# A decoder layer on one core: six gate loads, the operands around the FFN, and the last rows' statistics put elsewhere

## The chip, the core and the metric

The kernel runs on one core of a Trainium2 chip. The core has five engines that work from queues of their own: TensorE (PE, matmuls, into banks of PSUM), VectorE (DVE), ScalarE (ACT), GpSimd (POOL) and SyncE (SP), which only starts transfers; POOL starts transfers too. An instruction waits in its queue until its operands and its buffers are free, and what stands behind it on that engine waits with it. The metric is device time of the whole program in microseconds.

## What is computed

One decoder layer on x of 2048 rows by 1024 columns, float32:

```python
proj = x @ w_in                       # 4872 columns, split among the heads and gates
y_a = sliding_window_attention_with_sinks(aq, ak, av, sinks) @ w_attn_out
o = gated_delta_rule_chunked(dq, dk_, dv_, g, beta)      # behind a conv and SiLU
y_b = (rms_norm(o) * dn_norm_w * silu(dz)) @ w_dn_out
mix = (sigmoid(g_a) * y_a + sigmoid(g_b) * y_b) @ w_out
x = layer_norm(alpha * x + mix)                          # ln1
h = square(relu(x @ w_up)) @ w_down                      # 4096 hidden columns
x = layer_norm(alpha * x + h)                            # ln2
```

## The kernel before

Every matmul operand is split into a high and a low part: ScalarE copies the raw tile to the rounded type (hi), VectorE subtracts that from the raw tile (lo, called a remainder here). A product is then three matmuls per block, hi by hi, hi by lo, lo by hi.

Tokens go through in four quarters of 512. **Stage A** makes the projections, attention and the delta rule of all quarters, and stores y inputs (ya, yb) and gates (tg) to DRAM. The **y stage** takes a quarter at a time in eight blocks m of 128 columns; each has two products of 12 matmuls (L147). `prepare` loads ya and yb (L982), `load_y` a block's weights w (L1044, L1045), both on SP's queue for the first quarter; the two gates of a block come by POOL (L1021). VectorE multiplies by the gates, and L1100 is the product with w_out. `turn_rows` and `norm_steps` make ln1 and its transpose.

The **FFN's first half** is a loop over two token halves s and 16 pairs p of 128-column blocks. A pair is one level of a Strassen-like scheme: seven products n = 0 to 6 of 12 matmuls each (L1392) into the banks X, Z, X, Y, X, Z, X, on the sums T1 to T4 and blocks B11 to B22 of the tokens and sums S1 to S4 and blocks of the weights. n = 0, 1, 3 begin a bank anew, the others add on it. After n = 0, 1, 2 `keep` (L1348) copies the bank to SBUF, and the next product on the bank can't start before that copy is done. After n = 3 to 6 `out_block` (L1355 to L1357) adds, applies relu and squares. `h_sums` (L1368 to L1377) makes four sums S1 to S4 of a pair's blocks, and `store` (L1361) writes blocks and sums to DRAM (h). `x_operand` loads, copies and splits a token operand (L945, L950, L953); `up_weights` does that for weights and their sums (L1124 to L1157).

The **down stage** has groups g of hidden columns and, inside, four token quarters tq, again with seven products (L1518); each is added to the rows in SBUF by `add` (L1465), and the bank it reads is free after that. `hidden` loads what the first half stored (L1215), copies (L1222) and splits (L1226); `down_operand` does so for w_down (L1266 or L1268, L1271, L1273) through raw buffers lng, lnb and dr. In the last group `norm_out` (L1471 to L1487) makes ln2 of the rows of a quarter with ScalarE's accumulations and POOL's power and add; the last two rows of the last quarter go through `norm_steps` (L872 to L884) instead.

From the FFN on, the order on every engine is the order of the code. Helpers are generators: `go_on` advances each one in the list `ahead` by a step after every product, so the place where a helper enters `ahead` decides which instructions stand before and behind its own. In the stages before, PE's order is by code, and that of the others by priorities.

## Time and profile before

| what | us |
|---|---|
| median of three runs (2818.43 to 2823.88) | 2819.61 |
| profiled execution | 2823.9 |
| its span | 2822.2 |
| PE busy in it | 2744.7 |
| VectorE busy | 1916.0 |
| ScalarE busy | 1202.7 |
| POOL busy | 688.0 |

The profiled execution is the slowest of the three. PE is busy almost throughout, so the places to read are those where it stands, what releases it there, and the clock it is granted afterwards. Between stages the engines hand over to each other, and a share over the whole span doesn't show that; the timeline around a place does.

### The profile page before, as it was taken

How to read it: one execution, taken by the hardware profiler on the slowest of the kernel's cores; microseconds unless marked ns; L12 is line 12 of the kernel's file. 1: busy time of each engine (PE TensorE's matmuls, PEld its weight loads, DVE VectorE, ACT ScalarE, POOL GpSimd, SP SyncE). 2: the span in 40 equal slices, each digit the busy share in tenths (PEclk: the TensorE clock that was granted, in tenths of full speed). 3: DMA queues.
4: the chain of work that ended last, by engine and by line, in shares of the span. 5: the costliest groups of instructions: out<-in, count | busy, mean ns of one | idle time of the engine just before them, and what ended most of it. 6: DMA issues, size and time to landing. Idle time of an engine off the chain costs nothing. (4 is left out here: it accounts for less than half of the span.)

```text
span 2822.2 us, 37859 instructions
## 1 busy us (share of the span) xinstructions
PE 2744.7 (97%) x13509; PEld 2263.3 (80%) x13509; DVE 1916.0 (68%) x3032; ACT 1202.7 (43%) x2406; POOL 688.0 (24%) x913
## 2 busy tenths in 40 slices
PE   8999999999999999999999999999999999999996
PEld 6878888888888888788878788878887888888874
DVE  6875666466645674566766866698865777777787
ACT  4545443444344434323323555565555322223345
POOL 1022202230223032213462124448730000000015
PEclk9999999999999999999999999999999999999998
DMA  6785556354634464857787567789975644444443
GB/s 211 235 278 188 213 172 209 130 188 168 211 135 178 169 205 136 242 193 261 255 274 246 175 215 236 247 284 301 302 242 185 248 152 153 129 134 152 146 143 137
DMA packets 355083, 569.91 MB, mean 202 GB/s; under 512 B 42208, under 2 KB 236880, under 8 KB 354896
## 3 DMA queue, kind: packets, MB, share of 16 engines
q1 hardware_dynamic: 313616, 426.97, 46.5%
q0 software_dynamic: 41280, 140.54, 14.0%
q8 instruction: 106, 1.74, 0.2%
q14 instruction: 81, 0.66, 0.1%
HBM read 391.22 MB, written 176.19 MB: 201 GB/s over the span
## 5 line engine op out<-in xcount | busy, mean ns | idle before, releaser
L329 PE MATMUL pj<-x,w 128*128 128x512 f32 x3648 | 930.4, 399 | 4.6 <-DVE qs L723 2.5
L329 PEld LDWEIGHTS pj<-x,w 128*128 128x128 f32 x3648 | 662.3, 189 | 128.9 <-issue 2.9
L1518 PE MATMUL X<-x,w 128*128 128x512 f32 x1536 | 369.5, 393 | 13.7 <-DVE st L1477 7.0
L1392 PE MATMUL X<-x,w 128*128 128x512 f32 x1536 | 368.4, 392 | 12.1 <-ACT c L1348 11.7
L1518 PEld LDWEIGHTS X<-x,w 128*128 128x128 f32 x1536 | 290.0, 190 | 78.4 <-issue 14.5
L1392 PEld LDWEIGHTS X<-x,w 128*128 128x128 f32 x1536 | 289.7, 189 | 74.5 <-ACT c L1348 13.3
L1222 ACT ACTIVATE w<-w 128x1024 fp32r<-128x1024 f32 x96 | 101.5, 1058 | 251.8 <-DMA w<-h 251.8
L1136 DVE TENSOR_TENSOR w<-w,w 128x512 fp32r<-128x512 f32 x224 | 174.3, 789 | 16.2 <-ACT w L1132 15.9
L1392 PE MATMUL Z<-x,w 128*128 128x512 f32 x768 | 185.2, 390 | 0.0
L147 PE MATMUL b<-x,w 128*128 128x512 f32 x768 | 181.4, 396 | 3.2 <-ACT w L110 2.6
L1518 PE MATMUL Z<-x,w 128*128 128x512 f32 x768 | 184.4, 389 | 0.0
L111 DVE TENSOR_TENSOR w<-w,w 128x1024 fp32r<-128x1024 f32 x102 | 127.9, 1254 | 82.1 <-PE b L1100 44.0
L110 ACT ACTIVATE w<-w 128x1024 fp32r<-128x1024 f32 x102 | 107.8, 1057 | 171.1 <-DMA w<-in_w_dn_out_dram 84.7
L1478 POOL TENSOR_TENSOR st<-st,mh 128x1 f32<-128x1 f32 x14 | 7.6, 556 | 683.1 <-DVE st L1477 683.1
L147 PEld LDWEIGHTS b<-x,w 128*128 128x128 f32 x768 | 145.3, 191 | 33.8 <-ACT w L110 2.9
L1392 PEld LDWEIGHTS Z<-x,w 128*128 128x128 f32 x768 | 144.3, 188 | 30.0
L1518 PEld LDWEIGHTS Z<-x,w 128*128 128x128 f32 x768 | 144.2, 188 | 29.9
L1132 ACT ACTIVATE w<-w 128x512 fp32r<-128x512 f32 x224 | 135.9, 621 | 62.4 <-DVE w L1142 33.6
L1465 DVE SCALAR_TENSOR_TENSOR x<-x,X 128x1024 f32<-128x1024 f32 x96 | 117.0, 1219 | 66.1 <-PE X L1518 66.1
L1100 PE MATMUL b<-w,x 128*128 128x512 f32 x512 | 159.4, 392 | 0.0
L1226 DVE TENSOR_TENSOR w<-w,w 128x1024 fp32r<-128x1024 f32 x96 | 122.4, 1275 | 12.3 <-ACT w L1222 12.3
L414 DVE SCALAR_TENSOR_TENSOR acc<-cin,cw,acc 128x512 f32<-128x512 f32 x144 | 114.3, 794 | 15.9 <-ACT acc L412 13.5
(326 smaller groups left out, 4361.9 us busy)
## 6 DMA issues: line engine op xcount, KB each, us to landing
w<-whd SPq DMA_DIRECT2D x114, 512.0 KB, 3.3
w<-wld SPq DMA_DIRECT2D x114, 512.0 KB, 4.6
h<-c SPq DMA_DIRECT2D x224, 256.0 KB, 4.4
w<-h SPq DMA_DIRECT2D x96, 512.0 KB, 3.5
w<-in_w_up_dram SPq DMA_DIRECT2D x64, 512.0 KB, 5.5
w<-in_w_in_dram SPq DMA_DIRECT2D x38, 512.0 KB, 4.4
whd<-w SPq DMA_DIRECT2D x38, 512.0 KB, 3.1
wld<-w SPq DMA_DIRECT2D x38, 512.0 KB, 5.1
```

Source lines behind the costliest of these rows:

```text
L110: A.activation(hi, raw, AF.Copy)
L111: V.tensor_tensor(lo, raw, hi, ALU.subtract)
L147: PE.matmul(pp, lhsT=a[:, k0 + k, :], rhs=b[k // 4][:, k % 4, :], start=n == 0, stop=n == 3 * nk - 1)
L329: PE.matmul(pp, lhsT=a[:, k, :], rhs=b[k // 4][:, k % 4, :], start=n == 0, stop=n == 23)
L414: V.scalar_tensor_tensor(acc, cin[:, j:j + TQ], cw[:, 12 * j + gi:12 * j + gi + 1], acc, ALU.mult, ALU.add)
L1100: PE.matmul(accs[tb], lhsT=a[:, kg, ts_], rhs=b[:, k, :], start=kg == 0 and n == 0, stop=kg == 7 and n == 2)
L1132: A.activation(t[:, 0, :], src, AF.Copy)
L1136: V.tensor_tensor(l, raw[name], h, ALU.subtract)
L1226: V.tensor_tensor(parts[1], raw_, parts[0], ALU.subtract)
L1392: PE.matmul(dst, lhsT=l[:, ks], rhs=r[:, xs], start=first and k == 0 and m == 0, stop=k == 3 and m == 2, skip_group_check=not first)
L1465: V.scalar_tensor_tensor(dst, dst, 1.0 if (tq, half, ch) in touched else ALPHA, bank, ALU.mult, ALU.add)
L1518: PE.matmul(dst[:, j], lhsT=l[:, ks], rhs=r[:, k], start=first and k == 0 and m == 0, stop=k == 1 and m == 2, skip_group_check=not first)
```

## The change

Six places change. In the y stage of the first quarter, the gates of blocks 0 to 2 are loaded by SP, behind the weights of their block, instead of by POOL. In the FFN's first pair, operand B22 is loaded into four 128x512 tiles of the tag "c" in place of two 128x1024 slots of the weights, and T4 is copied a step later. The four sums of the pairs (0, 14) and (1, 15) are made by POOL, as those of (0, 15) were already. The first `hidden` of the down stage and its operands 0 to 5 enter `ahead` one product earlier. In the last quarter, all four row tiles take their statistics with bn_stats and go through `norm_steps`, and each is stored in two halves; `norm_out` loses its case for the end.

```diff
--- before.py
+++ after.py
@@ -940,7 +940,8 @@
         src = x_source(s, name)
         hi, lo = (t[:, i].rearrange("p k t -> p (k t)") for i in range(2))
         dst[name] = (hi, lo)
-        parts = [(raw, slice(i * D, i * D + D)) for i, raw in enumerate(raws)]
+        w = raws[0].shape[-1]
+        parts = [(raw, slice(i * w, i * w + w)) for i, raw in enumerate(raws)]
         for raw, cs in parts:
             q.dma_start(raw, src[:, cs])
         yield
@@ -1005,6 +1006,18 @@
                 A.activation(xt, ps_, AF.Copy)
                 G.dma_start(x1t_d[s][:, kh, th, :, tb * P:tb * P + P], xt)
 
+        def y_weights(m):
+            ms = slice(m * P, (m + 1) * P)
+
+            def load_y(raw):
+                wa = w_attn.rearrange("(j t d) c -> j d t c", j=2, t=4)
+                for j in range(2):
+                    nc.sync.dma_start(raw[64 * j:64 * j + 64, 0:4, :], wa[j][:, :, ms])
+                loads.append(nc.sync.dma_start(raw[:, 4:8, :], w_dn[:, ms].rearrange("(k p) c -> p k c", p=P)))
+
+            with (tc.issue_after(loads[-1].ins) if len(loads) < 20 else nullcontext()):
+                return weights(None, [NK, P], load=load_y)
+
         for q in range(NQ):
             t0 = q * TQ
             ys = ready
@@ -1018,8 +1031,14 @@
                 for i in range(2):
                     th = tgs[:, tgn % 6, :]
                     tgn += 1
-                    lastg = G.dma_start(th, tg_d[q][:, i * NK + m, :])
+                    if q > 0 or m > 2:
+                        lastg = G.dma_start(th, tg_d[q][:, i * NK + m, :])
                     gates.append(th)
+                wy = y_weights(m) if q == 0 else None
+                if q == 0 and m < 3:
+                    with tc.issue_after(loads[-1].ins):
+                        for i, th in enumerate(gates):
+                            loads.append(nc.sync.dma_start(th, tg_d[q][:, i * NK + m, :]))
                 if q == 0 and m == 6:
                     with tc.issue_after(lastg.ins):
                         G.dma_start(gt, ln1_g[0].partition_broadcast(P))
@@ -1036,16 +1055,7 @@
                 if lastq:
                     next(sums, None)
                     next(sums, None)
-                ms = slice(m * P, (m + 1) * P)
...
-                with (tc.issue_after(loads[-1].ins) if q == 0 and m >= 2 else nullcontext()):
-                    wh, wl = weights(None, [NK, P], load=load_y)
+                wh, wl = wy or y_weights(m)
                 for i in range(2):
                     yh, yl = ys[i]
                     pp = new(ps, [P, TQ], "b", 6)
@@ -1258,16 +1268,16 @@
         name = RIGHT[i]
         o = dn[0] % 8
         dn[0] += 1
-        while len(dx) <= o // 2:
-            dx.append(xslot(len(dx), (2, 2, 2, TQ)))
-        t = dx[o // 2][:, o % 2]
-        dst[name] = (t[:, 0], t[:, 1])
         if name in SUMS:
             nc.sync.dma_start(raw, wsum_d[g][:, SUMS[name]])
         else:
             nc.sync.dma_start(raw, wd[g][int(name[1]) - 1][int(name[2]) - 1])
         yield
         yield
+        if len(dx) <= o // 2:
+            dx.append(xslot(len(dx), (2, 2, 2, TQ)))
+        t = dx[o // 2][:, o % 2]
+        dst[name] = (t[:, 0], t[:, 1])
         A.activation(t[:, 0], raw, AF.Copy)
         yield
         V.tensor_tensor(t[:, 1], raw, t[:, 0], ALU.subtract)
@@ -1312,11 +1322,12 @@
 
         run(up_weights(0, all_wops[0]))
         load_up(1)
-        for name in ("B22", "T4"):
-            ahead.append(x_operand(0, name, xops[0], [flat(slot(F32)) for _ in range(2)], nc.sync, 2))
+        ahead.append(x_operand(0, "B22", xops[0], [new(sb, [P, TQ], "c", 11) for _ in range(4)], nc.sync, 2))
+        ahead.append(x_operand(0, "T4", xops[0], [flat(slot(F32)) for _ in range(2)], nc.sync, 3))
         go_on()
         side = side_work()
         part = None
+        GP = {(0, NP - 2), (0, NP - 1), (1, NP - 1)}
 
         halves, places = [], []
         BEGIN = [1, 2, 2, 3, 3, 4, 5, 5, 6, 7, 8, 9, 10, 11]
@@ -1363,7 +1374,7 @@
 
                 store = storing()
 
-                def h_sums(h=h, store=store, eng=G if turn_over else V):
+                def h_sums(h=h, store=store, eng=G if (s, p) in GP else V):
                     s1 = tile_c()
                     eng.tensor_tensor(s1, h["A21"], h["A22"], ALU.add)
                     store("S1", s1)
@@ -1397,10 +1408,8 @@
                     for _ in range(BEGIN.count(at)):
                         ahead.append(halves.pop(0))
                     go_on()
-                    if n == 0:
-                        ahead.append(hidden(0, 0, hops) if final else loaded.pop(0))
-                        if final:
-                            next(ahead[-1])
+                    if n == 0 and not final:
+                        ahead.append(loaded.pop(0))
                     if n == 6 and s * NP + p + 2 < 2 * NP:
                         load_up(s * NP + p + 2)
 
@@ -1429,12 +1438,13 @@
                         next(side, None)
                     elif part != "turn" and n < 6:
                         part = next(side)
-                    if final:
-                        if n == 0:
-                            lnc = [new(lnpool, [P, D], "lng", 1), new(lnpool, [P, D], "lnb", 1)]
-                        for i in {0: (0, 1), 3: (2, 3), 6: (4, 5)}.get(n, ()):
-                            ahead.append(down_operand(0, i, bops, lnc[i % 2].rearrange("p (k c) -> p k c", k=2)))
-                            next(ahead[-1])
+                    if at == 7 * NP - 1:
+                        ahead.append(hidden(0, 0, hops))
+                        next(ahead[-1])
+                        lnc = [new(lnpool, [P, D], "lng", 1), new(lnpool, [P, D], "lnb", 1)]
+                    for i in {-1: (0, 1), 2: (2, 3), 5: (4, 5)}.get(at - 7 * NP, ()):
+                        ahead.append(down_operand(0, i, bops, lnc[i % 2].rearrange("p (k c) -> p k c", k=2)))
+                        next(ahead[-1])
                 if final:
                     for steps in after:
                         run(steps)
@@ -1465,7 +1475,7 @@
             V.scalar_tensor_tensor(dst, dst, 1.0 if (tq, half, ch) in touched else ALPHA, bank, ALU.mult, ALU.add)
             touched.add((tq, half, ch))
 
-        def norm_out(r, t, end):
+        def norm_out(r, t):
             junk = new(sb, [P, D], "dr", 5)
             st_ = new(lnt, [P, 4], "st", 4)
             A.activation(junk, r, AF.Copy, accum_out=st_[:, 0:1])
@@ -1477,16 +1487,13 @@
             V.tensor_scalar(st_[:, 3:4], st_[:, 2:3], 1.0 / D, LN_EPS, ALU.mult, ALU.add)
             G.tensor_tensor(st_[:, 3:4], st_[:, 3:4], mh, ALU.pow)
             yield
-            if end:
-                V.scalar_tensor_tensor(r, junk, st_[:, 3:4], bt_, ALU.mult, ALU.add)
-                nc.sync.dma_start(out[t * P:t * P + P, :], r)
-                return
             A.activation(junk, junk, AF.Copy, scale=st_[:, 3:4])
             yield
             G.tensor_tensor(r, junk, bt_, ALU.add)
             ST.dma_start(out[t * P:t * P + P, :], r)
             yield
 
+        norms_ = []
         load_acc(0)
         for g in range(NG):
             bo = bops
@@ -1503,7 +1510,7 @@
                 end = last and tq == 3
                 tl = tiles_of(tq)
                 banks = {"X": new(ps, [P, 2, TQ], "X", 2), "Y": new(ps, [P, 2, TQ], "Y", 1), "Z": new(ps, [P, 2, TQ], "Z", 1)}
-                stats = [new(lnt, [P, 2, 6], f"bl{j}", 1) for j in range(2)] if end else None
+                stats = [new(lnt, [P, 2, 6], f"bl{j}", 1) for j in range(4)] if end else None
                 for n, (a, b, bank) in enumerate(SEVEN):
                     if a not in ho or b not in bo:
                         go_on()
@@ -1524,19 +1531,20 @@
                     add(tq, *((0, 0), (1, 1), (0, 1), (0, 0), (1, 1), (0, 1), (1, 0))[n], dst)
                     if g == 0 and tq < 3 and n == 1:
                         load_acc(tq + 1)
-                    if last and n == 5:
-                        ahead += [norm_out(acc[tq][:, j, :], tl[j], end) for j in range(2)]
-                    if end and n == 4:
+                    rows_ = [acc[tq][:, j, :] for j in range(4)]
+                    if last and not end and n >= 5:
+                        ahead += [norm_out(rows_[2 * (n - 5) + j], tl[2 * (n - 5) + j]) for j in range(2)]
+                    if end and n >= 3:
                         for j in range(2):
-                            V.bn_stats(stats[j][:, 1, :], acc[tq][:, 2 + j, TQ:])
-                    if last and n == 6:
-                        for j in range(2):
-                            r, t = acc[tq][:, 2 + j, :], tl[2 + j]
-                            if end:
-                                V.bn_stats(stats[j][:, 0, :], r[:, 0:TQ])
-                                ahead.append(norm_steps(r, gt, bt_, mh, out[t * P:t * P + P, :], stats[j], True))
-                            else:
-                                ahead.append(norm_out(r, t, end))
+                            half, ch = ((0, 0), (1, 1), (0, 1), (1, 0))[n - 3]
+                            V.bn_stats(stats[2 * half + j][:, ch, :], rows_[2 * half + j][:, ch * TQ:ch * TQ + TQ])
+                    if end and n >= 5:
+                        for j in range(2 * (n - 5), 2 * (n - 5) + 2):
+                            t = tl[j]
+                            if n == 6:
+                                run(norms_.pop(0))
+                            norms_.append(norm_steps(rows_[j], gt, bt_, mh, out[t * P:t * P + P, :], stats[j], True))
+                            next(norms_[-1])
                     if g == 0 and tq == 0 and n == 0:
                         ahead.append(down_operand(0, 6, bo, new(sb, [P, 2, TQ], "dr", 5)))
                         next(ahead[-1])
@@ -1545,8 +1553,9 @@
                         if i is not None:
                             ahead.append(down_operand(g + 1, i, bops, new(sb, [P, 2, TQ], "dr", 5)))
                             next(ahead[-1])
-        while ahead:
-            go_on()
+        assert not ahead
+        for steps in norms_:
+            run(steps)
 
 
 _INS = ["x", "w_in", "conv_w", "attn_sinks", "dn_a_log", "dn_dt_bias", "dn_norm_w", "w_attn_out", "w_dn_out", "w_out",
```

PE's instructions are the same, in the same order. Three places show what moves on the others. In the names, w is a weight tile, x a token or operand tile, c a copy or output block; the number behind it tells tiles apart.

SP's queue ahead of the first quarter's y stage, before:

```order
L982 DMA x_2165_11567<-ya_1_57 128x1024 x2
L982 DMA x_2165_11567<-yb_5_61 128x1024 x2
L1044 DMA w_11588<-in_w_attn_out_dram 64x4x128 x2
L1045 DMA w_11588<-in_w_dn_out_dram 128x4x128
L1044 DMA w_11629<-in_w_attn_out_dram 64x4x128 x2
L1045 DMA w_11629<-in_w_dn_out_dram 128x4x128
L1044 DMA w_11670<-in_w_attn_out_dram 64x4x128 x2
L1045 DMA w_11670<-in_w_dn_out_dram 128x4x128
```

The same stretch of SP's queue now:

```order
L983 DMA x_2165_11567<-ya_1_57 128x1024 x2
L983 DMA x_2165_11567<-yb_5_61 128x1024 x2
L1015 DMA w_11586<-in_w_attn_out_dram 64x4x128 x2
L1016 DMA w_11586<-in_w_dn_out_dram 128x4x128
L1041 DMA x_2168_11583<-tg_9_65 128x512 x2
L1015 DMA w_11627<-in_w_attn_out_dram 64x4x128 x2
L1016 DMA w_11627<-in_w_dn_out_dram 128x4x128
L1041 DMA x_2168_11583<-tg_9_65 128x512 x2
```

The loads tg, two for each block, stand behind the block's weights; before, they were on POOL's queue.

ScalarE's queue in the FFN's first pair, from the first copy out of bank X to the second, before (L950 copies B22 and T4):

```order
L1348 ACTIVATE c_14467<-X_14452 128x512
L1132 ACTIVATE w_14490<-w_14438 128x512
L1348 ACTIVATE c_14493<-Z_14454 128x512
L950 ACTIVATE x_2600_14446<-w_14442 128x1024
L950 ACTIVATE x_2600_14446<-w_14443 128x1024
L950 ACTIVATE x_2601_14449<-w_14444 128x1024
L950 ACTIVATE x_2601_14449<-w_14445 128x1024
L1132 ACTIVATE w_14511<-w_14489 128x512
L1348 ACTIVATE c_14515<-X_14452 128x512
```

The same stretch of ScalarE's queue now (L951 copies, L1359 is the copy out of a bank, L1142 the weights' copy):

```order
L1359 ACTIVATE c_14471<-X_14456 128x512
L1142 ACTIVATE w_14494<-w_14438 128x512
L1359 ACTIVATE c_14497<-Z_14458 128x512
L951 ACTIVATE x_2602_14448<-c_14442 128x512
L951 ACTIVATE x_2602_14448<-c_14443 128x512
L951 ACTIVATE x_2602_14448<-c_14444 128x512
L951 ACTIVATE x_2602_14448<-c_14445 128x512
L1142 ACTIVATE w_14515<-w_14493 128x512
L1359 ACTIVATE c_14519<-X_14456 128x512
L951 ACTIVATE x_2603_14453<-w_14446 128x1024
L951 ACTIVATE x_2603_14453<-w_14447 128x1024
```

B22's copies are four of half the width ahead of the second copy out of X; T4's two copies have moved behind it.

SP's queue at the end of the FFN's first half, from the store of a block of pair (1, 14) on, before (c tiles 19597, 19557, 19625 and 19628 are the sums):

```order
L1361 DMA h_1_2575_14391<-c_19578 256x1x256
L1361 DMA h_1_2575_14391<-c_19597 256x1x256
L1361 DMA h_1_2575_14391<-c_19557 256x1x256
L1215 DMA w_19604<-h_0_2560_14376 128x1024
L1268 DMA lng_19608<-in_w_down_dram 128x2x512
L1266 DMA lnb_19609<-ws_2576_14392 128x1024
L1361 DMA h_1_2575_14391<-c_19625 256x1x256
L1361 DMA h_1_2575_14391<-c_19628 256x1x256
```

SP's queue there now (c tiles 19611, 19565, 19632 and 19635 are the sums):

```order
L1372 DMA h_1_2575_14391<-c_19586 256x1x256
L1225 DMA w_19590<-h_0_2560_14376 128x1024
L1274 DMA lng_19592<-in_w_down_dram 128x2x512
L1272 DMA lnb_19593<-ws_2576_14392 128x1024
L1372 DMA h_1_2575_14391<-c_19611 256x1x256
L1372 DMA h_1_2575_14391<-c_19565 256x1x256
L1372 DMA h_1_2575_14391<-c_19632 256x1x256
L1372 DMA h_1_2575_14391<-c_19635 256x1x256
```

The loads of hidden rows and of the two operand raws, lng and lnb, moved ahead of the four stores of sums.

## Rows read from the trace of the kernel before

**Rows 1.** The page's first part: busy us, share of the span, instructions

```profile
PE 2744.7 (97%) x13509; PEld 2263.3 (80%) x13509; DVE 1916.0 (68%) x3032; ACT 1202.7 (43%) x2406; POOL 688.0 (24%) x913
```

**Rows 2.** The list of PE's waits: us in total, times, longest us

```profile
PE X L1392 <- ACT c L1348: 11.7, 4, 6.0
```

**Rows 3.** Timeline of PE, first y products; start, us, operation, [idle before <-releaser]

```profile
1169.57 0.73 PE L147 MATMUL b<-x,w 128*128 128x512 f32 x2 [2.65 <-ACT w L110]
1170.83 44.87 PE L147 MATMUL b<-x,w 128*128 128x512 f32 x190 [0.53 <-DVE w L111]
```

**Rows 4.** Timeline of ScalarE, the first y weights' copy

```profile
1168.46 1.06 ACT L110 ACTIVATE w<-w 128x1024 fp32r<-128x1024 f32 x1 [3.33 <-DMA w<-in_w_attn_out_dram]
```

**Rows 5.** Timeline of POOL and of SP's queue, before the y stage

```profile
1151.80 3.25 POOL L1021 DMA_DIRECT2D x<-tg  x6
1154.42 1.41 SPq L1044 DMA_DIRECT2D w<-in_w_attn_out_dram  x2
```

**Rows 6.** Timeline of PE, fifth product of the FFN's first pair

```profile
1559.34 4.81 PE L1392 MATMUL X<-x,w 128*128 128x512 f32 x12 [5.99 <-ACT c L1348]
```

**Rows 7.** Timeline of ScalarE, FFN's first pair

```profile
1553.39 0.63 ACT L1132 ACTIVATE w<-w 128x512 fp32r<-128x512 f32 x1 [7.56 <-PE Y L1392]
```

**Rows 8.** Timeline of PE, ScalarE, SP: last pair, first down quarter

```profile
2162.64 4.41 PE L1392 MATMUL X<-x,w 128*128 128x512 f32 x12 [2.16 <-ACT c L1348]
2179.92 3.00 PE L1518 MATMUL X<-x,w 128*128 128x512 f32 x12 [1.77 <-DVE r L1465]
2187.57 4.58 PE L1518 MATMUL X<-x,w 128*128 128x512 f32 x12 [1.93 <-DVE r L1465]
2158.16 1.06 ACT L1222 ACTIVATE w<-w 128x1024 fp32r<-128x1024 f32 x1 [2.49 <-DMA w<-h]
2153.10 0.58 SPq L1215 DMA_DIRECT2D w<-h  x1
2184.74 0.33 SPq L1266 DMA_DIRECT2D dr<-ws  x1
```

**Rows 9.** Windows: length, busy us of five engines, granted clock, DMA share, GB/s

```profile
1169.50:1174.00 4.50, 3.90 (x10) 2.79 (x11) 3.25 (x4) 2.54 (x4) 0.00 (x0) 0.63 1.18 253
1559.30:1563.00 3.70, 3.66 (x9) 2.89 (x10) 3.70 (x5) 0.63 (x1) 0.00 (x0) 0.50 0.35 142
2162.60:2167.00 4.40, 4.36 (x13) 3.46 (x14) 1.36 (x2) 2.21 (x3) 0.00 (x0) 0.65 0.16 57
2187.50:2191.50 4.00, 3.93 (x10) 3.12 (x11) 2.25 (x3) 1.06 (x1) 0.00 (x0) 0.57 0.96 376
1861.80:1871.10 9.30, 8.01 (x36) 6.32 (x35) 9.07 (x7) 5.99 (x9) 9.13 (x4) 1.00 1.07 345
```

**Rows 10.** Timeline of VectorE, then SP's queue, FFN's first pair

```profile
1554.05 0.69 DVE L1136 TENSOR_TENSOR w<-w,w 128x512 fp32r<-128x512 f32 x1 [5.41 <-ACT w L1132]
1557.85 4.62 DVE L953 TENSOR_TENSOR x<-w,x 128x1024 fp32r<-128x1024 f32 x4
1543.05 1.12 SPq L945 DMA_DIRECT2D w<-x1t  x2
```

**Rows 11.** Transfers issued at 1505 to 1560: count, KB each, median us to landing

```profile
w<-x1t SPq DMA_DIRECT2D x2, 512.0 KB, 5.2
```

**Rows 12.** Timeline of VectorE after the sums of pair (0, 14)

```profile
1846.21 0.69 DVE L1142 TENSOR_TENSOR w<-w 128x512 f32<-128x512 f32 x1 [2.78 <-DMA w<-in_w_up_dram]
```

**Rows 13.** Timeline of VectorE while POOL makes sums

```profile
1863.98 4.27 DVE L934 TENSOR_TENSOR x<-r,x 128x1024 fp32r<-128x1024 f32 x2 [0.18 <-ACT x L932]
```

**Rows 14.** Timeline of VectorE and POOL, last rows

```profile
2815.64 2.47 DVE L1481 SCALAR_TENSOR_TENSOR x<-dr,st,lnb 128x1024 f32<-128x1024 f32 x2
2806.64 0.57 POOL L1487 DMA_DIRECT2D out_dram<-x  x1 [0.30 <-POOL x L1486]
```

**Rows 15.** Transfers issued from 2790 on: count, KB each, median us to landing

```profile
out_dram<-x SPq DMA_DIRECT2D x4, 256.0 KB, 2.0
out_dram<-x SPq DMA_DIRECT2D x2, 512.0 KB, 2.7
```

5 lines of the change are left out of this document (removed).

## The prediction

> **What bounds the kernel now.** I read the page's busy times first: PE, the matmul engine, is busy for 97% of the span [rows 1], and its matmuls are the same in number and order after the change. So the change can only buy back time in which PE stands still or runs at a lower clock. The list of PE's waits says where it stands still; its longest group is the FFN's first half waiting for ScalarE's copies out of PSUM, 11.7 us with one wait of 6.0 [rows 2]. Then I went through the places one by one in the timelines.
>
> Place A, the first products of the first quarter's y stage: two waits, 2.65 and 0.53 us [rows 3]. ScalarE's copy of the first weights ends the first; it waited 3.33 us for their load and began at 1168.46 [rows 4]. That load was issued at 1154.42, behind six gate loads that POOL had issued at 1151.80 [rows 5].
>
> Place C, the fifth product (n=4) of the FFN's first pair, waits 5.99 us for the copy L1348 [rows 6]. ScalarE was held 7.56 us by a weight copy whose slot PE still read [rows 7], and then did four operand copies ahead of that L1348.
>
> Place E, the last pair and the first quarter of the down stage: waits of 2.16, 1.77 and 1.93 us [rows 8].
>
> Each of the three is followed by a stretch at a lower granted clock: 0.63 after A, 0.50 after C, 0.65 and 0.57 in E [rows 9]. These lie between the two levels of 1.2 and 2.4 GHz: part of the stretch ran at the lower one. Busy time times the missing share is the loss: 3.90 x 0.37 = 1.44 us (A), 3.66 x 0.50 = 1.83 (C), 4.36 x 0.35 + 3.93 x 0.43 = 3.2 (E). So a wait that goes takes about half its own length or more with it. The pools are 2.65 + 0.53 + 1.44 = 4.6 us at A, 5.99 + 1.83 = 7.8 at C, 5.86 + 3.2 = 9.1 at E.
>
> **The change part by part.**
>
> *A: gates behind weights.* Six gate loads leave POOL's queue and stand on SP's, two each behind the weights of m = 0, 1, 2. Before, six gates of 256 KB were in flight ahead of the first weights; at the 345 GB/s that the queues moved in the turn between the token halves [rows 9] they are 4.6 us of transfer. The first weights could be copied at 1168.46; without that traffic I put it at 1163 to 1165, copy and remainder done by about 1166.5, before PE gets there at 1166.9 (2.65 us ahead of the first row of rows 3). Waits and clock go: 4.6. I leave 0.3 for the second weights, now behind two gates: **4.3 us** (2 if the first weights still land 2 us late, 4.6 at best).
>
> *C: operand B22 into four half-width tiles, T4 later.* The weight copy's slot is no longer shared with the raw operand tiles, so the 7.56 us hold goes. B22's load was issued at 1543.05 and took 5.2 us to land [rows 10, 11]; four copies of half the width (0.63 us each, as the weight copy of that shape in rows 7) end near 1551, and the L1348 copy that PE waits for ends near 1552, ahead of PE's need at 1553.3 (the start in rows 6 less the wait). T4's two copies now stand behind it. What is late next is VectorE. Before, it stood 5.41 us until 1554.05, so from 1548.6, and ended its four remainders at 1562.5 [rows 10]: 8.4 us of work from 1554.05 on. Starting at 1548.6 it would end near 1557, and with an add and weight steps that the new order puts ahead of T4's remainders (four of 0.69) near 1560. PE needs these at the seventh product: at 0.229 us per matmul (44.87 less 1.44 us over 190 [rows 3]) a product of 12 takes 2.74, so at 1553.3 + 5.5 = 1558.8. I leave a wait of 1.1 with its clock. 7.8 - 1.1 = **6.7 us** (4.5 if that wait is 3 with its clock, 7.8 if none).
>
> *D: the sums of pair (0, 14) go to POOL.* Four adds leave VectorE there. It then has nothing to do: its next work waits 2.78 us for a weight load and starts at 1846.21 [rows 12]. So the freed time buys nothing. The stores of the sums come later and SP's loads for the second token half stand behind them: **0** (-2 to +0.5).
>
> *E: the down stage's first operands one product earlier, last sums on POOL.* The first load of the hidden rows was issued at 2153.10 behind two stores of sums; now it stands ahead of them, at about 2151.8. ScalarE's copy of it began at 2158.16 and held the copy that PE waited for [rows 8]; it and the two operand copies behind it shift by 1.3 us and, with two fewer stores in flight, a little more. The 2.16 us wait falls to about 0.7. The four sums (0.69 each on VectorE) stood ahead of the add that the second wait names; on POOL they don't, so the 1.77 us go. The third, 1.93, depends on an operand's remainders ahead of the add, and I leave 1.2. New: SP issues the last operand's load behind the sums' stores. On POOL four sums took 9.13 us in the turn [rows 9], against 4 x 0.69 on VectorE. Before, that load went out at 2184.74 and nobody waited. With sums from about 2170.5 to 2179.6 it goes out near 2181 and its remainder is done near 2188, when PE needs it: I put 1.0 there, up to 4.5 if the sums start late. Waits left: 0.7 + 1.2 + 1.0 = 2.9 of 5.86, gain 3.0; the clock loss falls from 3.2 to near nothing, since in the turn the clock stayed at 1.00 over 9.30 us in which PE stood for 1.29 [rows 9]. Gain **6.1 us** (3 to 8).
>
> *POOL against VectorE.* While POOL added, two VectorE remainders took 4.27 us [rows 13], against 4.62 for four of that size [rows 10]: both at work cost VectorE about 1 us per sum. That is in my waits of 1.2 and 1.0. The Trainium skill ("SBUF — State Buffer", "Who interferes with whom") says that VectorE and GpSimd share a pair of ports, and that the second to issue "fully blocks" when VectorE has two SBUF inputs. The row agrees in direction; by the page each sum would cost its whole length, 2.3 us instead of about 1. Rival 3 has the time.
>
> *Tail.* The last four rows' statistics all come from VectorE's bn_stats; the ScalarE passes L1471 and L1475 of two rows and VectorE's steps between them go. Before, VectorE ended with two L1481 from 2815.64 on (2.47 us together), then a 512 KB store of 2.7 us [rows 14, 15]. After, the powers of the last rows sit on POOL behind the quarter before's last store, issued at 2806.64 for 0.57 [rows 14]; VectorE's second step of the first row waits for that until about 2807.9, some 1 us. Then seven steps (L1481 took 1.24 each; in two halves I put 1.33) and small ones end near 2817.7, 0.4 earlier; the last store is 256 KB, 2.0 us [rows 15]. **1.0 us** (0 to 2.4).
>
> Sum: 4.3 + 6.7 + 0 + 6.1 + 1.0 = 18.1 us. The profiled execution took 2823.9 (span 2822.2), so it would read 2805.8; it was the slowest of three, and from the median of 2819.6 the forecast is 2801.5. The poor ends add up to 2 + 4.5 - 2 + 3 + 0 = 7.5 (2812), the good ends to 23.3 (2796).
>
> **The rivals.**
>
> 1. *Part is given back.* The last operand at E lands 4.5 us late, or VectorE's chain at C 3 us late, and a lower clock follows. For it: both stand behind an engine that loses speed while the other works. Gain 8 to 12, so 2808 to 2812.
>
> 2. *Waits are only replaced.* ScalarE works in order. If its copies of the first hidden rows and operands still sit in front of the copy PE needs, E gains only the sums' 1.8 us; if the gate loads on SP wait for a buffer that stage A's last gate frees near 1174.5, the second weights are held, and PE, which needs them 24 matmuls or 5.5 us after its start at 1166.9, stands until they have landed (5.2 us, as in rows 11) and been split, near 1183, 10 us. Against it: the slot the gates use was free for POOL's loads at 1151.80 [rows 5]. With both, A gives 4.6 - 10 = -5, E 2, C 6.7, tail 1: a gain of about 4 to 5, so 2815, around no change.
>
> 3. *Slower: POOL's sums block VectorE.* If each of the eight moved sums stopped VectorE for its whole 2.3 us (9.13 over four [rows 9]), that is 18.4 us at the two ends of the token halves, where PE already waits for VectorE. If all of it reached PE, with a clock loss of 0.31 us per us as at C (1.83 over 5.99), it would cost 24: 2819.6 - 18.1 + 24 = 2825.5. It eats the gain from 1.7 us of PE's waiting per sum on. For it: both engines work on the same tiles there. Against it: the trace shows about 1 us of VectorE time per sum, and pair 14's sums fall where VectorE waits anyway. The page named above states this rule.
>
> 4. *The change doesn't do what it says:* the first weights still land last because ya and yb, a megabyte each, are ahead of them either way. Then A gives 0 and the time is 2806.
>
> **How the numbers follow.** Forecast 0.62; rival 1, 0.2; rival 4, 0.06; rival 2, 0.08; rival 3, 0.04. A measurement of this kernel can tell about 0.2%, 5.6 us, from no change. Faster by more than that: forecast, rivals 1 and 4, 0.88; within it: rival 2, 0.08; slower: rival 3, 0.04. The range reaches from a little under the good ends, 2795, to the slow end of rival 1 and the poor ends, 2812; outside lie rivals 2 and 3.
>
> **What would show it.** A: no PE wait at L147's start, weights' copy before 1166. C: the slot wait of L1132 gone, B22's copies ahead of the L1348 copy, PE wait under 2 us at the seventh product. E: the 1.77 wait gone, the first under 1; if instead a wait of over 3 us stands at the seventh product of the down stage, rival 1 holds. D: waits of the turn as before; if they grow by over 4 us, rival 3. Wrong altogether if any stretch that I call unchanged moves by over 3 us.

## The result, and the profile after

The changed kernel takes 2802.49 us (median; 2801.48 to 2804.84), the kernel before on the same chip 2821.74. The ratio on record is 0.9926, 95% interval 0.9912 to 0.9941 (these two medians alone give 0.9932): faster, by about 0.7%. The forecast was 2801.5, with a range of 2795 to 2812, a gain of 18.1 us; the medians differ by 19.3.

The page's busy line of after answers to [rows 1]: PE has the same 13,509 matmuls and is busy for 8.4 us less.

```profile
PE 2736.3 (98%) x13509; PEld 2258.8 (81%) x13509; DVE 1910.8 (68%) x3034; ACT 1198.7 (43%) x2400; POOL 691.5 (25%) x915
```

The list of PE's waits, after (us in total, times, longest). The group of [rows 2] has gone from 11.7 us in four waits to 5.0 in three, and the top of the list is now waits in the down stage's last fifth.

```profile
PE X L1525 <- DVE st L1487: 7.8, 3, 3.3
PE X L1403 <- ACT c L1359: 5.0, 3, 2.4
PE X L1525 <- DVE r L1475: 2.7, 2, 2.0
```

Place by place, timelines of after. PE at the start of the y stage and in the FFN's first pair:

```profile
1165.70 43.82 PE L147 MATMUL b<-x,w 128*128 128x512 f32 x192
1543.66 2.88 PE L1403 MATMUL X<-x,w 128*128 128x512 f32 x12
1549.50 5.72 PE L1403 MATMUL X<-x,w 128*128 128x512 f32 x24 [0.24 <-DVE c L1366]
```

A has no wait left; [rows 3] had 2.65 and 0.53. At C the fifth product (at 1543.66), which waited 5.99 us [rows 6], starts without a wait, and only 0.24 is left at the seventh, for an add. The next rows are ScalarE's copy of A's first weights, which [rows 4] had at 1168.46 (1.0 of the difference is stage A's earlier end); then, in C, the weight copy that was held for 7.56 us in [rows 7], B22's four narrow copies, and the copy out of X that the fifth product waits for; then VectorE's two remainders of T4:

```profile
1163.80 1.06 ACT L110 ACTIVATE w<-w 128x1024 fp32r<-128x1024 f32 x1 [1.77 <-DMA x<-tg]
1536.20 0.62 ACT L1142 ACTIVATE w<-w 128x512 fp32r<-128x512 f32 x1
1538.92 2.18 ACT L951 ACTIVATE x<-c 128x512 fp32r<-128x512 f32 x4
1541.53 0.58 ACT L1359 ACTIVATE c<-X 128x512 f32<-128x512 f32 x1
1545.81 2.35 DVE L954 TENSOR_TENSOR x<-w,x 128x1024 fp32r<-128x1024 f32 x2
```

PE, then POOL's first of four sums, then SP's queue, at the turn into the down stage (E):

```profile
2146.96 3.02 PE L1403 MATMUL X<-x,w 128*128 128x512 f32 x12 [1.21 <-ACT c L1359]
2166.98 3.01 PE L1525 MATMUL X<-x,w 128*128 128x512 f32 x12 [0.69 <-DVE r L1475]
2174.70 7.33 PE L1525 MATMUL X<-x,w 128*128 128x512 f32 x24 [1.99 <-DVE r L1475]
2156.58 1.29 POOL L1379 TENSOR_TENSOR c<-c,c 128x512 f32<-128x512 f32 x1 [93.17 <-DVE w L1236]
2157.68 5.07 SPq L1372 DMA_DIRECT2D h<-c  x5
2164.32 0.33 SPq L1272 DMA_DIRECT2D dr<-ws  x1
```

The waits of [rows 8] (2.16, 1.77, 1.93) are 1.21, none and 0.69, and a new one of 1.99 stands at the seventh product of the first down quarter. Its operand is the one whose load SP issued at 2164.32, behind five stores.

To compare whole kernels I cut PE's timeline into stretches from the start of one product to the start of another. A goes from stage A's end to the first out projection, Y from there to the FFN's first product, C from there to the second pair's second product. D is the turn from pair 15's sixth to pair 17's second product, E from the last pair's second product to the second quarter's second product of the down stage. "Down" is from there to the last product's start, "tail" the rest. The two stretches of the FFN that lie between hold 281.3 to 283.0 and 266.6 to 271.3 us everywhere. The first two rows are the unchanged kernel.

| us | A | Y | C | D | E | down | tail | span |
|---|---|---|---|---|---|---|---|---|
| before | 48.6 | 326.8 | 29.9 | 32.1 | 48.0 | 599.7 | 22.4 | 2822.2 |
| null_before | 49.9 | 325.3 | 29.7 | 34.3 | 47.3 | 600.4 | 22.3 | 2825.2 |
| after | 43.4 | 323.4 | 22.3 | 34.5 | 44.4 | 599.9 | 21.4 | 2803.1 |
| gates_pool | 49.2 | 326.4 | 22.2 | 34.2 | 41.1 | 601.6 | 20.6 | 2811.0 |
| b22_slots | 43.4 | 323.5 | 28.9 | 34.7 | 42.1 | 600.6 | 21.5 | 2812.9 |
| t4_early | 43.8 | 321.0 | 23.2 | 34.7 | 45.2 | 599.9 | 21.4 | 2804.0 |
| p14_vector | 44.6 | 325.2 | 22.2 | 36.6 | 42.0 | 600.4 | 21.4 | 2806.3 |
| pool_stores | 43.7 | 322.9 | 22.2 | 33.0 | 43.4 | 600.5 | 21.2 | 2797.6 |
| late_hidden | 43.4 | 322.3 | 22.2 | 34.6 | 47.3 | 600.6 | 21.4 | 2810.7 |
| p31_vector | 43.7 | 320.8 | 22.2 | 33.3 | 41.6 | 601.2 | 20.8 | 2799.2 |
| raw6 | 43.6 | 322.2 | 22.4 | 35.0 | 44.5 | 600.8 | 20.8 | 2807.3 |
| add_first | 43.4 | 323.3 | 22.5 | 34.2 | 45.0 | 603.5 | 21.7 | 2807.1 |
| combo | 43.8 | 323.1 | 22.4 | 34.6 | 41.3 | 603.7 | 20.8 | 2802.3 |
| combo_stores | 43.4 | 321.8 | 22.1 | 35.0 | 41.1 | 603.7 | 21.8 | 2806.0 |

From the profile of before to that of after the 19.1 us come from A 5.2, Y 3.3, C 7.6, E 3.5, the tail 1.0 and 1.0 ahead of A; D gives back 2.4, and 0.1 is rounding and the rest. The 1.0 ahead of A says little: stage A ends anywhere from 1162.1 to 1169.3 us in the twelve profiles of changed kernels.

### The profile page after: what moved, and what is told of

Same layout as the page of the kernel before. It is cut to its first block, busy times and chain, and to the rows that moved or that the text cites. A ratio compares the mean times of both kernels' runs of the same rounds, so it can differ in the third digit from the quotient of the medians.

```text
span 2803.1 us, 37882 instructions
## 1 busy us (share of the span) xinstructions
PE 2736.3 (98%) x13509; PEld 2258.8 (81%) x13509; DVE 1910.8 (68%) x3034; ACT 1198.7 (43%) x2400; POOL 691.5 (25%) x915
## 4 chain that ended last, share of the span: by engine, by line
PE 83%; DVE 7%; DMA 4%; issue 2%; ACT 2%; POOL 1%; SPq 0%; DVEq 0%; ACTq 0%; POOLq 0%
PE pj L329 25%; PE X L1403 12%; PE X L1525 11%; PE Z L1403 6%; PE Z L1525 5%; PE b L1110 5%; PE b L147 5%; PE Y L1403 3%; PE Y L1525 3%; PE d L554 2%; DMA w<-in_w_in_dram 1%; DVE prod L542 1%; DVE qs L543 1%; PE at L779 1%; PE d L488 1%
## 5 line engine op out<-in xcount | busy, mean ns | idle before, releaser
L1525 PEld LDWEIGHTS Z<-x,w 128*128 128x128 f32 x768 | 144.1, 188 | 29.9
L1403 PEld LDWEIGHTS Z<-x,w 128*128 128x128 f32 x768 | 143.9, 188 | 29.9
L1142 ACT ACTIVATE w<-w 128x512 fp32r<-128x512 f32 x224 | 135.9, 621 | 48.3 <-DVE w L1152 26.8
```

Source lines behind the costliest of these rows:

```text
L1142: A.activation(t[:, 0, :], src, AF.Copy)
L1403: PE.matmul(dst, lhsT=l[:, ks], rhs=r[:, xs], start=first and k == 0 and m == 0, stop=k == 3 and m == 2, skip_group_check=not first)
L1525: PE.matmul(dst[:, j], lhsT=l[:, ks], rhs=r[:, k], start=first and k == 0 and m == 0, stop=k == 1 and m == 2, skip_group_check=not first)
```

## The experiments

### How far the unchanged kernel differs from itself: null_before

Nothing is edited.

> The kernel before, once more, for a second profile of it. The profiles of before and after differ by 3.4 us between the first out projection and the start of the FFN, where PE waits nowhere and the change has no instruction: 326.8 us before, 323.4 after. If that belongs to the kernels, this profile shows 326.8 again; if it is a matter of the execution, it may show 323 to 327. Time 2821.7 within 0.2% by either.

It took 2825.88 us, ratio 1.000 (0.999 to 1.001), and Y came to 325.3, between the two answers. Single stretches are less steady than the whole: A differs by 1.3 us between the two profiles of before, Y by 1.5, D by 2.2. By its time alone no edit below can be told from the changed kernel, as every interval overlaps 0.9912 to 0.9941; what the runs say of causes is read from waits and stretches, with one profile for each kernel.

### Place A: gates_pool

```diff
-                    if q > 0 or m > 2:
-                        lastg = G.dma_start(th, tg_d[q][:, i * NK + m, :])
+                    lastg = G.dma_start(th, tg_d[q][:, i * NK + m, :])
-                if q == 0 and m < 3:
-                    with tc.issue_after(loads[-1].ins):
-                        for i, th in enumerate(gates):
-                            loads.append(nc.sync.dma_start(th, tg_d[q][:, i * NK + m, :]))
```

> The changed kernel with the six gate loads of blocks 0 to 2 back on POOL's queue, all else as changed. My theory: the loads in flight ahead of the first weights were the whole wait, so the first y quarter takes 49 us again in place of 44.0, PE waits about 2.65 us for the first weights, and the time is 2807.5. Rival: what helped is that the weights are called for earlier in the code; then the quarter stays at 44 to 45 and the time at 2802.5.

2808.79 us, ratio 0.9943 (0.9928 to 0.9958), where the changed kernel had 0.9926. A is back at 49.2, and so is its wait (gates_pool, PE's waits):

```profile
PE b L147 <- ACT w L110: 2.3, 1, 2.3
```

The gates ahead of the weights were the cause of A's loss; rival 4 falls.

### Place C: b22_slots and t4_early

b22_slots gives B22's raw values two of the weight slots again and leaves T4 where the change put it; t4_early leaves B22 in its own tiles and starts T4 one step earlier, as before.

```diff
-        ahead.append(x_operand(0, "B22", xops[0], [new(sb, [P, TQ], "c", 11) for _ in range(4)], nc.sync, 2))
+        ahead.append(x_operand(0, "B22", xops[0], [flat(slot(F32)) for _ in range(2)], nc.sync, 2))
```

```diff
-        ahead.append(x_operand(0, "T4", xops[0], [flat(slot(F32)) for _ in range(2)], nc.sync, 3))
+        ahead.append(x_operand(0, "T4", xops[0], [flat(slot(F32)) for _ in range(2)], nc.sync, 2))
```

> The changed kernel with B22's raw tiles back in two weight slots; T4's copies stay late. The first FFN pair and the product behind it took 29.8 us in two profiles of before and 22.2 in four of changed kernels. My theory: the shared slot held ScalarE 7.56 us, and that was the most of it; so the hold comes back, less T4's two copies: 27 to 28 us, time 5 us over the changed kernel's. Rival: what helped is that fewer copies stand ahead of the copy that PE waits for; then 22 to 24.

> The changed kernel with T4 copied a step earlier, as before, ahead of the copy out of X that PE waits for; B22 stays in its own tiles. By the shared slot: ScalarE gets 2 us more work ahead of that copy, which then ends about 0.4 us after PE's need: 22.2 to 23 us for that stretch, time as the changed kernel's. By the rival, the order of the copies: a wait of 2 us or more with its clock, 25 us or more.

b22_slots: 2813.83 us, ratio 0.9951 (0.9935 to 0.9967), C 28.9. Timelines of ScalarE and PE in b22_slots:

```profile
1544.30 0.63 ACT L1142 ACTIVATE w<-w 128x512 fp32r<-128x512 f32 x1 [7.56 <-PE Y L1403]
1548.37 5.49 PE L1403 MATMUL X<-x,w 128*128 128x512 f32 x12 [4.10 <-ACT c L1359]
```

The 7.56 us of [rows 7] are back to the digit, and with them 6.6 of C's 7.6 us, a little more than I expected. The shared slot was the cause. t4_early: 2806.56 us, ratio 0.9936 (0.9917 to 0.9954), C 23.2. Its PE timeline shows what T4's place is worth, a wait of about 1 us:

```profile
1542.10 3.06 PE L1403 MATMUL X<-x,w 128*128 128x512 f32 x12 [1.10 <-ACT c L1359]
```

### Place D: p14_vector

```diff
-        GP = {(0, NP - 2), (0, NP - 1), (1, NP - 1)}
+        GP = {(0, NP - 1), (1, NP - 1)}
```

> The changed kernel with the sums of pair (0, 14) back on VectorE. The stretch at the turn of the token halves took 32.1 us before and 34.5 after. My theory: the late stores of these sums hold SP's loads for the second half, so the turn goes back to 32.1 and the time to 2800.1. Rival: the turn is set by the sums of pair (0, 15), on POOL in both kernels, and by chance; then 34 to 35 and 2802.5.

2803.67 us, ratio 0.9925 (0.9911 to 0.9940). After the first profiles I had laid D's 2.4 us on pair 14's sums on POOL. With these sums back on VectorE, D is 36.6, not 32. That theory falls: the sums' engine does not decide the turn, and the unchanged kernel itself shows 32.1 and 34.3 there. The timelines show where the 2.4 us are. PE at the turn's third wait, before and after:

```profile
1874.54 3.02 PE L1392 MATMUL X<-x,w 128*128 128x512 f32 x12 [2.22 <-ACT c L1348]
1858.30 4.55 PE L1403 MATMUL X<-x,w 128*128 128x512 f32 x12 [2.41 <-ACT c L1359]
```

The turn's waits grew by 0.8 us in all, and the 12 matmuls behind this one took 1.5 longer. PE's granted clock over D is 1.00 in both profiles of before, 0.95 in after and eight others, 0.91 in p14_vector, and 1.00 in pool_stores and p31_vector. Why it falls in ten of twelve profiles of changed kernels stays open: null_before stood for 2.67 us at the same place and kept 1.00.

### Place E: late_hidden, p31_vector, pool_stores

The change has two parts here, the earlier loads and the sums on POOL. late_hidden puts the hidden rows and the operands back by one product and leaves the sums on POOL; p31_vector does the opposite.

```diff
-                    if n == 0 and not final:
-                        ahead.append(loaded.pop(0))
+                    if n == 0:
+                        ahead.append(hidden(0, 0, hops) if final else loaded.pop(0))
...
-                    for i in {-1: (0, 1), 2: (2, 3), 5: (4, 5)}.get(at - 7 * NP, ()):
+                    for i in {0: (0, 1), 3: (2, 3), 6: (4, 5)}.get(at - 7 * NP, ()):
```

```diff
-        GP = {(0, NP - 2), (0, NP - 1), (1, NP - 1)}
+        GP = {(0, NP - 2), (0, NP - 1)}
```

> The changed kernel with the first hidden rows and the operands 0 to 5 of the down stage taken one product later, as before; the last sums stay on POOL. The entry took 48.0 and 47.3 us before and 44.4, 41.1, 42.0 in three profiles with the changed code. My theory: the earlier place removed the 2.16 us wait of the fifth product with its clock loss, so that comes back: 45 to 46.5, time 3 us more. Rival: the sums alone were worth it; then 41 to 44.

> The changed kernel with the last pair's sums back on VectorE. My theory: four adds of 0.69 us ahead of the adds that free PE's banks bring the 1.77 us wait at the third product of the down stage back, while the 0.8 to 2.0 us wait at the seventh goes, since its operand's load no longer stands behind POOL: the entry takes 42 to 44 us and the time doesn't move. Rival 3 of the prediction, sums on POOL block VectorE for their whole length: the entry gets shorter than 40.5.

late_hidden: 2812.4 us, ratio 0.9947 (0.9930 to 0.9965), E 47.3, as in the kernel before and more than I expected. p31_vector: 2801.8 us, ratio 0.9918 (0.9899 to 0.9937), E 41.6, under my 42 to 44 and shorter than in after. PE at E in late_hidden, at the fifth product of the last pair and the third and fifth of the down stage:

```profile
2151.45 4.61 PE L1403 MATMUL X<-x,w 128*128 128x512 f32 x12 [1.81 <-ACT c L1359]
2166.95 2.97 PE L1525 MATMUL X<-x,w 128*128 128x512 f32 x12
2176.10 4.32 PE L1525 MATMUL X<-x,w 128*128 128x512 f32 x12 [3.46 <-DVE r L1475]
```

and VectorE in p31_vector, a weight remainder, the four sums, then the add that the 1.77 us wait of [rows 8] names:

```profile
2153.48 1.23 DVE L1236 TENSOR_TENSOR w<-w,w 128x1024 fp32r<-128x1024 f32 x1 [0.31 <-ACT w L1232]
2154.66 0.69 DVE L1379 TENSOR_TENSOR c<-c,c 128x512 f32<-128x512 f32 x1
2155.39 0.69 DVE L1381 TENSOR_TENSOR c<-c,c 128x512 f32<-128x512 f32 x1
2156.00 0.68 DVE L1385 TENSOR_TENSOR c<-c,c 128x512 f32<-128x512 f32 x1
2156.77 0.69 DVE L1388 TENSOR_TENSOR c<-c,c 128x512 f32<-128x512 f32 x1
2157.38 1.22 DVE L1475 SCALAR_TENSOR_TENSOR r<-r,X 128x1024 f32<-128x1024 f32 x1
```

In p31_vector the sums still stand ahead of the add, and PE hardly waits for it (0.2 us): with the hidden rows early they fit in front. In late_hidden the wait at the third product is gone too, by the sums on POOL alone. But there the time comes back two products later, 3.46 us where [rows 8] had 1.93: the add in question stands behind the remainders of two operands whose loads go out as late as before, 24.7 us into E (25.1 before), and the fifth product starts 34.8 us into E (35.4 before). So either part removes the wait at the third product, and only the earlier loads shorten E; the sums on POOL by themselves add nothing to it.

The third edit asks about the new wait of 1.99: pool_stores sends the stores of POOL's sums out on POOL's own queue.

```diff
-                        nc.sync.dma_start(h_d[g][s][:, :, LEFT.index(name), k2, :], t.rearrange("p (u c) -> p u c", u=2))
+                        q.dma_start(h_d[g][s][:, :, LEFT.index(name), k2, :], t.rearrange("p (u c) -> p u c", u=2))
...
+                own = storing(G if (s, p) in GP else nc.sync)
-                def h_sums(h=h, store=store, eng=G if (s, p) in GP else V):
+                def h_sums(h=h, store=own, eng=G if (s, p) in GP else V):
```

> The changed kernel with the stores of all POOL-made sums (three pairs) issued from POOL's own queue in place of SP's. My theory: at the turn and at the entry of the down stage SP's loads stand behind these stores, so both give: the turn 32 or less (-2.4), and at the entry the wait of 1.99 us at the seventh product with its clock loss of 1.7 goes (-3.7): 2796.4. Rival: the last operand waits for its buffer, not for SP's queue, and POOL loses time with issuing; then the entry stays at 44.4 us and the time at 2800 to 2803.

2801.58 us, ratio 0.9917 (0.9903 to 0.9932), E 43.4. SP's queue, POOL's last two sums and VectorE's two remainders beside them, in pool_stores:

```profile
2153.28 0.60 SPq L1225 DMA_DIRECT2D w<-h  x1
2160.54 0.32 SPq L1272 DMA_DIRECT2D dr<-ws  x1
2156.13 1.42 POOL L1386 TENSOR_TENSOR c<-c,c 128x512 f32<-128x512 f32 x1
2158.45 1.40 POOL L1389 TENSOR_TENSOR c<-c,c 128x512 f32<-128x512 f32 x1
2156.92 1.72 DVE L1283 TENSOR_TENSOR x<-lng,x 128x1024 fp32r<-128x1024 f32 x1 [1.15 <-ACT x L1281]
2158.56 2.39 DVE L1283 TENSOR_TENSOR x<-lnb,x 128x1024 fp32r<-128x1024 f32 x1
```

No store stands on SP's queue ahead of the load of the seventh operand (dr), yet it goes out only at 2160.54. The list of SP's waits names what it waited for, in pool_stores and then in after, the landing of a store:

```profile
SPq L1272 <- DMA h<-c: 6.5, 1, 6.5
SPq L1272 <- DMA h<-c: 0.9, 1, 0.9
```

Its raw tile lies where block A21 was, in which the second sum (S3) is made, and that sum's store has to land first. In after this is the last thing that held the load, 0.9 us longer than SP's queue. The wait at the seventh product has gone, but one of 2.01 stands two products earlier, for VectorE, whose two remainders took 1.72 and 2.39 us instead of 1.2.

### The seventh operand's load: raw6

So I gave that operand a place of its own.

```diff
-                        ahead.append(down_operand(0, 6, bo, new(sb, [P, 2, TQ], "dr", 5)))
+                        ahead.append(down_operand(0, 6, bo, xslot(5, (4, 2, TQ), F32)[:, 0]))
```

> The changed kernel with one edit: the raw values of the seventh operand (T4) of the first half's down stage get a place that is free since the sixth product of the last pair, not the ring of 512-column tiles where the last sums of the FFN still stand. Theory: the 1.99 us that TensorE waits at the first quarter's last product come from that buffer alone (SyncE was free 10 us earlier). Then its load goes out by about 2156 instead of 2164, the wait at that product is under 0.3 us, the stretch from the last pair's second product to the second quarter's second product is 44.4 - 2.0 - 0.5 of clock = about 42 us, and the time 2 to 2.5 us under the changed kernel's: 2801.5 to 2802.5 where the kernel before takes 2826. Rival: the load is held by something else (the queue of SyncE, or its transfer is slow next to the others); then it goes out at 2162 to 2165 again, the wait stays at 1.3 to 2.4 us and the time at 2803 to 2805.

2806.59 us (2827.27 for the kernel before beside it), ratio 0.9921 (0.9901 to 0.9942), E 44.5: no gain. SP's queue in raw6:

```profile
2163.20 5.18 SPq L1372 DMA_DIRECT2D h<-c  x5
2168.43 0.60 SPq L1225 DMA_DIRECT2D w<-h  x1
2169.13 0.41 SPq L1272 DMA_DIRECT2D x<-ws  x1
```

The load still goes out behind the five stores, which wait for POOL's sums, 27.9 us into E where after has 26.9. My theory, the buffer alone, falls; the time is nearer the rival's, though its wait is not there. At the seventh product PE no longer stands, since it has stood at the fifth (PE, then VectorE ahead of the add, raw6):

```profile
2173.12 4.38 PE L1525 MATMUL X<-x,w 128*128 128x512 f32 x12 [3.24 <-DVE r L1475]
2168.18 1.23 DVE L1283 TENSOR_TENSOR x<-lng,x 128x1024 fp32r<-128x1024 f32 x1 [2.86 <-ACT x L1281]
```

So two causes stand in a row at that load: the stores ahead of it in the queue (raw6), and, without them (pool_stores), its buffer. Both removed, with the sums still on POOL, was not run. And which operand's chain ends last in E differs from profile to profile.

### The last fifth of the down stage, and all together: add_first, combo, combo_stores

The largest group of PE's waits in after lies in the last fifth of the down stage, in rows that the change leaves as they were. add_first does the adds there ahead of the statistics; combo joins it to raw6 and p31_vector; combo_stores is combo with pool_stores.

```diff
+                    if last:
+                        add(tq, *((0, 0), (1, 1), (0, 1), (0, 0), (1, 1), (0, 1), (1, 0))[n], dst)
                     go_on()
...
-                    add(tq, *((0, 0), (1, 1), (0, 1), (0, 0), (1, 1), (0, 1), (1, 0))[n], dst)
+                    if not last:
+                        add(tq, *((0, 0), (1, 1), (0, 1), (0, 0), (1, 1), (0, 1), (1, 0))[n], dst)
```

> The changed kernel with one edit: in the last fifth of the down stage VectorE adds a product to the rows first and does the statistics and remainders of that step afterwards. Theory: the three waits of 1.2, 3.3 and 3.3 us at products of the last fifth, which the trace lays on VectorE's statistics, are adds standing behind that work; then they fall to under 1 us in all, the clock stays up there (4.24 and 4.58 us for 12 matmuls become 3.0), and the time is 6 to 10 us under the changed kernel's: 2794 to 2798 where the kernel before takes 2826. Rival: VectorE is simply behind there, and what no longer waits for an add waits for a remainder; then the waits of the last fifth sum to 5 us or more and the time is within 2 us of the changed kernel's, 2802 to 2806.

> The two edits of the runs raw6 and add_first together, and the sums of the last pair back on VectorE (those of the first half's two last pairs stay on GpSimd). If all three act as in the runs by themselves, the turn into the down stage takes 40 to 41.5 us instead of 44.4 (no wait at the last product, 0.3 at the second quarter's first), the waits of the last fifth are under 1 us, and the time is 2791 to 2796 where the kernel before takes 2826. If the early loads' gain and the seventh operand's are one and the same, the turn stays at 41.5 to 43; if the last fifth only changes its waits, the time is 2799 to 2802.

> The run combo with one more edit: the eight stores of the sums that stay on GpSimd go out on GpSimd's own queue. Theory: at the turn between the halves SyncE's queue no longer holds the up-weights' load behind stores that wait for sums, so the stretch from pair 15's sixth product to pair 17's second is about 33 us instead of 34.5, and the time 1 to 1.5 us under the run combo's. Rival: the stores held nothing and the turn varies by itself from 32 to 36.6 us; then the load of up-weights in the turn lands at the same moment as in combo and the two times agree within 1 us.

add_first: 2810.04 us, ratio 0.9936 (0.9910 to 0.9961); its "down" is 3.6 us longer. PE's waits in add_first:

```profile
PE X L1525 <- DVE x L1475: 11.3, 3, 3.8
```

The 7.8 us for statistics and 1.4 for an add became 11.3 us for adds: the rival's mechanism, VectorE simply behind there, holds, with a time over its range. combo: 2806.58 us, 0.9924 (0.9901 to 0.9946), with E at 41.3 as expected and "down" at 603.7, so the rest of its theory falls with add_first's. combo_stores: 2809.05 us, 0.9932 (0.9911 to 0.9953), with D at 35.0 against combo's 34.6 and a granted clock of 0.95 there in both: taking the stores off SP's queue did not shorten the turn. No kernel here can be told from the changed one as faster: the intervals of p31_vector and pool_stores, the two with the lowest ratios, overlap its own.

## Why the prediction was right, point by point

**A: 5.2 measured, 4.3 forecast, 4.6 at best.** The mechanism is shown (gates_pool). The term was too small: without its two waits, A before still takes 48.6 - 3.2 = 45.4 us against 43.4 for the same 192 matmuls. So the lower clock and its surroundings cost 2.0 us (an estimate: the difference), where I had 1.44 from a window of 4.5 us. And the 0.3 us I left for the second weights did not come.

**C: 7.6 measured, 6.7 forecast, 7.8 at best.** The held slot was the cause (b22_slots). The step that failed is the wait of 1.1 for VectorE's remainders at the seventh product. I had T4's remainders end 17.7 us behind the FFN's first product (1560 less 1542.3); they end 15.4 us behind it (1545.81 + 2.35 less 1532.78), before the seventh product's turn at 1549.26, and that product waits 0.24 us for an add alone. The place I gave T4 was right and worth about 1 us (t4_early); the chain ahead of it was shorter than I had it.

**D: -2.4 in the profiled pair, 0 forecast, -2 at worst.** A term just outside its range. What it left out is the clock: I took the waits alone and read a clock of 1.00 in the turn from [rows 9], and most of the 2.4 is a clock of 0.95 over D. The edit named in the term is not the cause, since undoing it makes D longer, not shorter (p14_vector); whether the rest of the change is, the runs don't show.

**E: 3.5 measured, 6.1 forecast, 3 at worst.** The mean of the six profiles whose E is coded as in after (after, gates_pool, b22_slots, t4_early, p14_vector, add_first) is 43.3, that of the two of before 47.6, so 4.3 is the better figure; the six spread from 41.1 to 45.2. Two steps failed. First, the wait of 1.0 at the seventh product: it is 0.79 to 2.54 in the six, 1.99 in after. I had seen the stores ahead of the load, but not the buffer that holds it without them. Second, "the clock loss falls from 3.2 to near nothing": in the three profiles where PE waits 1.99 to 2.54 us at the seventh product, the 24 matmuls from there take 7.22 to 7.33 us, in the three where it waits 0.79 to 1.63 they take 5.69 to 5.72. E is 44.4 to 45.2 us in the first three and 41.1 to 42.1 in the others, so this is most of its spread, and none of it was in my sum. The step on the 1.77 us was right as far as it went (late_hidden has no such wait), but worth nothing alone, and the earlier loads remove the wait as well (p31_vector). The first wait, forecast at 0.7, is 1.21 in after and 0.54 to 0.94 in the other five.

**POOL against VectorE.** Rival 3 did not decide: POOL's sums took 1.28 to 1.74 us at pairs 14 and 31 of after, not 2.3, and in pair 14 VectorE, whose two remainders took 3.08 us instead of 1.28, still stood for 3.75 behind them. In two rows the price can be read: in pool_stores the remainder from 2156.92 shares 0.63 us with a sum and is 0.50 longer than 1.22, the next shares 1.29 us and is 1.17 longer. That agrees with the Trainium skill ("SBUF — State Buffer", "Who interferes with whom"), by which the one that comes second is held until the other is done. So in these two rows the price is about the overlap, not the sum's whole length as I put it in rival 3, and what matters is who waits for VectorE in it.

**Tail: 1.0 measured, 1.0 forecast.** The second step of VectorE's first rows and of its last in after:

```profile
2789.94 1.41 DVE L883 SCALAR_TENSOR_TENSOR x<-x,rs,lnb 128x512 f32<-128x512 f32 x2 [0.46 <-POOL rs L877]
2798.50 1.41 DVE L883 SCALAR_TENSOR_TENSOR x<-x,rs,lnb 128x512 f32<-128x512 f32 x2
```

The wait for POOL's power is there, 0.46 us instead of about 1, and the last pass is 1.41 for one row tile where [rows 14] had 2.47 for two. The parts came out otherwise than forecast: VectorE ends 18.2 us behind the last product's start (18.3 before), so 0.1 earlier and not 0.4, and the program ends 3.2 us behind VectorE (4.1 before), which gives 0.9 where I had 0.7 from the smaller last store. No run undoes this edit alone.

**Outside the terms.** Y, which I left out of the sum as unchanged, gave 3.3 us, and by the prediction's own last sentence that is a miss. The sum came out near because A, C and Y were better by 5.1 together and D and E worse by 5.0: the mechanisms of A and C are shown, but that the total fits is in part luck.

## What to carry to other kernels

When a load comes late, list everything that it waits for, its place in the queue and the last reader of its buffer (here a store that had to land); lifting either alone gained nothing that can be measured. When a change has two parts at one place, run each alone, and look at the waits behind the one that goes: the moved sums alone removed a wait, which then stood two products later, and the gain was the loads'. A reordering pays where the waited-for engine has slack (C's 7.6 us), and moves the wait where it has none (the last fifth of the down stage).

## What the runs showed that I had not expected

The out projection's matmuls run faster after the change, though no instruction of theirs is touched. Groups of PE's instructions by operands (ns of one: least, median, most), before:

```profile
L1100 PE MATMUL b<-w,x x512: 389/392/396, 1215.5 to 1541.8; 128*128 128x512 f32 x171
L1100 PE MATMUL b<-w,mgl x256: 397/397/397, 1216.0 to 1542.1; 128*128 128x512 f32 x128
```

and after:

```profile
L1110 PE MATMUL b<-w,x x512: 389/389/389, 1209.4 to 1532.3; 128*128 128x512 f32 x171
L1110 PE MATMUL b<-w,mgl x256: 389/389/389, 1209.8 to 1532.6; 128*128 128x512 f32 x128
```

256 x 8 ns and 512 x 3 ns are 3.6 us, and Y gained 3.3 in this pair: PE is busy there for 4.0 us less and stands for 0.7 more. In all profiles PE's busy time in Y is 322.0 and 321.3 us before and 316.9 to 319.6 in the twelve of changed kernels. The null run shows the 397 again, and every kernel built on the changed one has a median of 389 (single ones of 397 in pool_stores). gates_pool has it too; its Y stayed long, as PE was busy there for 319.6 us against 318.0 in after and stood for 6.8 against 5.4. So it belongs to the program, not to the execution. The one thing that I find to link the change to this loop is memory: the two statistics tiles that the last rows gained stand ahead of the tile mgl and push it on by 128 bytes in each partition. All kernels built on the changed one share that shift, so no run separates it, and the single slow ones in pool_stores speak against it as the whole cause; the kernel before with a dead tile of that size would tell. The cause stays open.
